# ScalarE's order written out in two MLPs, early loads of f, and sums of x pinned behind the last row block

## The chip, the core and the metric

The kernel runs on one core of a Trainium2 chip. Its engines are TensorE (PE; PEld are its weight loads), VectorE (DVE), ScalarE (ACT), GpSimd (POOL) and SyncE (SP), whose queue issues all DMAs here. The metric is the device time of one execution in microseconds (us), the median of several runs.

## The reference

Two decoder layers over 1024 tokens of width 1024 in float32. Each layer has a mixer (gated linear attention beside sparse attention in the first, a spatial-gating MLP in the second) and then a dense MLP of hidden width 4096. The change is in the two dense MLPs:

```python
def _squared_relu_mlp(x, w1, w2):
    h = jax.nn.relu(x @ w1)
    return (h * h) @ w2

f = _squared_relu_mlp(_rms_norm(h, norm_g[layer, 2]), ffn_w1[layer], ffn_w2[layer])
h = h + _rms_norm(f, norm_g[layer, 3])
```

## The kernel before

Every product is made in three passes of a high and a low part: `split` copies the high part with ScalarE (`acopy`, line 138) and takes the low part as a difference with VectorE (`sub`, line 148). A matmul has 128 x 128 weights and 512 columns; `mm` (line 162) records them all.

`ffn` (line 360) computes f = relu(x w1) squared and then f w2, both by a scheme of seven products in place of eight for 2 x 2 blocks (`SEVEN`, line 351). It has these stages:

- **The start.** The boundary of the stage before gives x in rows of 128 tokens, eight blocks, each normalised, transposed by TensorE and split into `xT`. The first four column blocks of w1 are multiplied in the plain way (`f1`, line 381), and meanwhile the sums of x that the seven products need are made from `xT`: `whole` (line 437) adds high and low part of a slice, `sums_y` (line 440) makes ten VectorE instructions for each of four slices k. `split1(2)` between them splits the third column block of w1.
- **The pair loop** (line 651), pairs q = 2 to 15 of column blocks of w1. A pair has seven units u = 0 to 6 (`unit1`, line 489) of 12 matmuls. The units of one pair share three banks; several units add onto a bank whose earlier value has been copied out by then: units 2 and 4 onto that of unit 0. ScalarE copies the banks of units 0, 2 and 3, and applies relu and square for unit 6; VectorE adds units 1, 4 and 5. In each unit the next pair's weights are prepared (`prep_pair`, line 470: a difference or sum where the scheme wants one, the ScalarE copy, the VectorE difference). `fetch_pair` (line 460) loads 1 MB of w1 for pair q+2, and `scale_pair` (line 465) multiplies it by the norm's gain, eight ScalarE copies, two each in units 3 to 6 by the code. Results go to DRAM (`fbuf`), with their sums (`sums_f`, line 514).
- **The second product** (line 693): 28 steps, a group of two pairs (steps 0 to 6) and three groups of four pairs, each with seven steps. A step multiplies four row blocks (`rows2`, line 592) and prepares the next step's weights and f (`prep2`, line 557). f comes back from DRAM through `fetch_f` (line 541) into a ring of five places, the weights through `fetch_w2` (line 548). Group 0 copies banks out with ScalarE or adds with VectorE, by the unit; the other groups add.
- **The end**: the plain product of the first four column blocks and the boundary to the next stage. Its operands come in through `of_last` (line 613).

The program is scheduled at build time. Each engine executes its queue in order; which instruction stands where in the queue is the scheduler's choice by its own clock, unless `tc.keep_in_program_order` pins an instruction behind the one traced before it on its engine. `keep` (line 143) does that while `fixed` is true, from the pair loop to the end of the second product. Before, TensorE's matmuls and VectorE's additions, differences and the relu-square step were pinned there; ScalarE's copies were not. DMA issues are pinned in neither kernel.

Of the kernel before, what the change touches and what calls it, by code (L numbers as in the profile page):

```python
# [117 lines left out]
def tile_trunk(ctx, tc, x, norm_g, ffn_w1, ffn_w2, e_w_in, e_w_out, gla_w_gate, gla_b_gate,  # L118
# [15 lines left out]

    act, dve, pool, pe = nc.scalar, nc.vector, nc.gpsimd, nc.tensor

    def acopy(o, i, **kw):
        act.activation(o, i, AF.Copy, **kw)  # L138


    fixed = [False]

    def keep(ins):
        if fixed[0]:
            tc.keep_in_program_order(ins)

    def sub(o, a, b):
        keep(dve.tensor_tensor(o, a, b, op=OP.subtract))  # L148
# [211 lines left out]
    def ffn(l, hsrc, hdst, gi, nxt):  # L360
# [74 lines left out]
        tmp = Ring(stg[4:] + [bnd.reg(o, 512) for o in (6, 8, 10, 12)])  # L435

        def whole(o, name, k):
            add(o.f, Y[name].f[:, 0, k], Y[name].f[:, 1, k])

        def sums_y(k):  # L440

# [47 lines left out]
        def unit1(q, u):  # L489
            x, y, which, begin, _, _ = SEVEN[u]  # L490
            b = 3 * (q % 2) + (0 if which == 0 else 1 if u == 1 else 2)
            w, xh = live(pairs[q, x]), Y[y]
            for k in range(4):
                for i, (a, v) in enumerate(PASS):
                    mm(bank[:, b, :], w.r[:, a, k, :], xh.r[:, v, k, :],
                       begin and k == 0 and i == 0, k == 3 and i == 2)
            pb = bank[:, b, :]
            if u in (0, 2, 3):
                hf[q, ("11", 0, "21", "22")[u]] = r = ring.next()
                acopy(r.f, pb)  # L500
            elif u == 6:
                hf[q, "12"] = r = ring.next()
                act.activation(r.f, pb, AF.Relu)
                act.activation(r.f, r.f, AF.Square)
                store(q, "12", r)
            else:
                name = {1: "11", 4: "22", 5: "21"}[u]
                r = live(hf[q, name])
                add(r.f, r.f, pb)
                keep(dve.scalar_tensor_tensor(r.f, r.f, 0.0, r.f, op0=OP.max, op1=OP.mult))  # L510
                if u != 5:
                    store(q, name, r)
# [13 lines left out]
        groups = [[2, 3]] + [list(range(4 + 4 * i, 8 + 4 * i)) for i in range(3)]  # L526
        wraw = [shaped(v, (2, 2, 512)) for v in (raw2, rawt)]
        T1 = [bnd.reg(o, 512) for o in (8, 10, 12, 6)]
        stage = Ring([bnd.reg(o, 512) for o in (14, 16, 0, 2, 4)])
        setA, setB = (X[h].ring(0, 8, 2, 512).views for h in range(2))  # L530
        setC = HS + [ws.reg(0, 2, 512)]
# [9 lines left out]
        def fetch_f():  # L541
            if len(loaded) < len(queue):
                q, name = queue[len(loaded)]
                r = stage.next()
                nc.sync.dma_start(r.f, frow(q, name))
                loaded.append(r)

# [9 lines left out]
        def prep2(g, u):  # L557

            slots = sets[g, u]
            for j, q in enumerate(groups[g]):  # L560
# [20 lines left out]
                def of_f(j=j):  # L581
                    o = slots[2 * j + 1]
                    src = loaded[taken[0]]
                    taken[0] += 1
                    yield from halves(live(src), o[:, 0], o[:, 1])
                    if (g, u) != (0, 0):
                        fetch_f()

                yield of_w()
                yield of_f()  # L590
# [59 lines left out]
        fixed[0] = True  # L650
        for q in range(2, NP):
            if q == NP - 1:
                for j in range(2):
                    for name in ("11", "12", "21", "22"):
                        fetch_w2(0, j, name)
                first = iter(list(prep2(0, 0)))
            for u in range(7):
                work = []
                if q + 1 < NP:
                    work.append(prep_pair(q + 1, u))  # L660
                elif u >= 3:
                    work.append(next(first))
                for w in work:
                    next(w)
                unit1(q, u)
                for w in work:
                    all_of(w)
                sums_f(q - 1 if u < 6 else q, u)
                if q == NP - 1 and u in (1, 2):
                    fetch_f()  # L670
                if u == 0:
                    fetch_pair(q + 2)
                if u >= 3:
                    scale_pair(q + 2, (2 * u - 6, 2 * u - 5))
# [1 line left out]
        acc = sb.F("acc", NT * D, slot="acc")  # L676
        acc_of = [acc.reg(4 * t, D) for t in range(NT)]
        wraw += [sa.F(f"w2raw{i}", 2, 2, 512, slot=f"w1{i}") for i in (1, 0)]
        for j in (2, 3):
            for name in ("11", "12", "21", "22"):  # L680
                fetch_w2(1, j, name)
        sums_f(NP - 1, 0)
        for _ in range(2):
            fetch_f()
        order = [(g, u) for g in range(len(groups)) for u in range(7)]
        ws2 = sb.R("w2b", 3 * D, slot="w2b")
        WS = ws.ring(0, 4, 2, 512).views + ws2.ring(0, 3, 2, 512).views
        wT = {(i // 2, i % 2): s for i, s in enumerate(WS + [HS[6]])}
        rest = [of_last(k, c, i) for i, k, c in
                [(i, "w", c) for c in range(2) for i in range(2)]  # L690
                + [(0, "h", c) for c in range(4)] + [(i, "w", c) for c in (2, 3) for i in range(2)]
                + [(1, "h", c) for c in range(4)]]
        for s, (g, u) in enumerate(order):
            steps = list(prep2(*order[s + 1])) if s + 1 < len(order) else []
            n = len(steps)
            for rb in range(4):
# [13 lines left out]
                    all_of(w)  # L710
                if s == 0 and rb == 0:
                    sums_f(NP - 1, 1)
                    for _ in range(5 - len(loaded) + taken[0]):
                        fetch_f()
        fixed[0] = False
        assert not rest
        load_gpost(gi + 1)
# [901 lines left out]
    i = 0  # L1619
# [50 lines left out]
```

## Time and profile before

| | us |
|---|---|
| median of three runs | 2587.97 (2586.36 to 2588.24) |
| the profiled execution | 2585.08 |
| its span | 2583.3 |
| TensorE busy | 2504.6 (97%) |
| VectorE busy | 1784.9 (69%) |
| ScalarE busy | 1280.9 (50%) |
| DMA, share of 16 engines | 33.3% |

A busy TensorE is not TensorE at its peak: matmuls overlap, one takes 393 ns in the record and a new one starts every 227 ns or so. What counts are the stretches in which it starts none. The first MLP lies from about 690 to 1385 us of the span, the second from about 1900 to the end.

### The profile page before, as it was taken

To read this page: it belongs to the slowest core of one execution; us is meant where nothing else is said; L and a number is where in the kernel's file an instruction comes from. 1 tells how busy PE (TensorE), PEld (TensorE's weight loads), DVE (VectorE), ACT (ScalarE), POOL (GpSimd) and SP (SyncE) were. 2 spreads that over 40 slices of the span, in tenths; PEclk is the share of its full clock that TensorE was granted. 3 is DMA by queue.
4 is the path that set the end of the run, shared out by engine and by line. 5 is a ranking of instruction groups with operands and counts; after the bars stand their busy time and mean duration, and the time that the engine had idled before them with its cause. 6 is when DMAs were issued, how large, how long until landed. Compare 5 with 4: busy or idle time off the path is not lost. (4 is left out here: it accounts for less than half of the span.)

```text
span 2583.3 us, 33390 instructions
## 1 busy us (share of the span) xinstructions
PE 2504.6 (97%) x12130; PEld 2086.6 (81%) x12130; DVE 1784.9 (69%) x3107; ACT 1280.9 (50%) x2503; POOL 297.8 (12%) x204
## 2 busy tenths in 40 slices
PE   8999999999999998999999999999999999999998
PEld 7888888888777777788887888888887777778886
DVE  5576478887776665887874248665667666588786
ACT  5656378787664444544454132233356544454442
POOL 2321122332400000000020011100020000000003
PEclk9999999999999999999999999999999999999999
DMA  4122110002534445454442111121243444544534
GB/s 131 51 66 81 58 41 34 25 18 90 188 106 139 135 144 203 131 163 163 138 157 98 33 42 41 41 82 49 74 139 106 135 139 142 202 136 162 162 122 163
DMA packets 191694, 279.56 MB, mean 108 GB/s; under 512 B 14388, under 2 KB 97576, under 8 KB 191528
## 3 DMA queue, kind: packets, MB, share of 16 engines
q1 hardware_dynamic: 191528, 277.42, 33.3%
q8 instruction: 95, 1.56, 0.2%
q14 instruction: 71, 0.58, 0.1%
HBM read 198.72 MB, written 78.64 MB: 107 GB/s over the span
## 5 line engine op out<-in xcount | busy, mean ns | idle before, releaser
L162 PE MATMUL bank<-base_x 128*128 128x512 f32 x1920 | 453.0, 393 | 14.6 <-ACT base_x L138 12.0
L162 PEld LDWEIGHTS bank<-base_x 128*128 128x128 f32 x1920 | 362.3, 189 | 97.7 <-ACT base_x L138 13.9
L154 DVE TENSOR_TENSOR ffb_acc<-ffb_acc,bank 128x512 f32<-128x512 f32 x224 | 152.9, 686 | 101.4 <-PE bank L162 100.1
L138 ACT ACTIVATE base_x<-base_bnd 128x512 fp32r<-128x512 f32 (+1 forms) x193 | 120.9, 639 | 184.3 <-DMA base_bnd<-fbuf 110.5
L162 PE MATMUL bank<-base_x,ffa_w 128*128 128x512 f32 x864 | 205.6, 395 | 3.5 <-ACT base_bnd L390 1.9
L162 PE MATMUL bank<-base_x,ffa_w1n 128*128 128x512 f32 x816 | 195.2, 394 | 2.0 <-DVE ffa_w1n L148 2.0
L162 PEld LDWEIGHTS bank<-base_x,ffa_w 128*128 128x128 f32 x864 | 163.6, 191 | 40.1 <-ACT base_bnd L390 2.8
L162 PE MATMUL bank<-base_x,mv_w 128*128 128x512 f32 x768 | 185.9, 393 | 0.8 <-DVE nsq_qq L1368 0.8
L260 POOL TENSOR_TENSOR ffb_acc<-ffb_acc,base_bnd 128x1024 f32<-128x1024 f32 x15 | 37.2, 2486 | 1277.5 <-ACT base_bnd L210 1269.2
L162 PEld LDWEIGHTS bank<-base_x,ffa_w1n 128*128 128x128 f32 x816 | 152.5, 189 | 33.4 <-DVE ffa_w1n L148 2.5
L162 PEld LDWEIGHTS bank<-base_x,mv_w 128*128 128x128 f32 x768 | 140.7, 188 | 28.4 <-DVE nsq_qq L1368 1.0
L148 DVE TENSOR_TENSOR base_x<-bank,base_x 128x512 fp32r<-128x512 f32 x204 | 135.5, 682 | 26.1 <-ACT base_x L138 24.9
L138 ACT ACTIVATE base_x<-bank 128x512 fp32r<-128x512 f32 x204 | 117.5, 598 | 50.1 <-PE bank L244 31.7
L148 DVE TENSOR_TENSOR base_x<-base_bnd,base_x 128x512 fp32r<-128x512 f32 (+1 forms) x185 | 127.2, 700 | 20.3 <-ACT base_x L138 20.3
L162 PE MATMUL bank<-base_x,ffb_hTb 128*128 128x512 f32 x480 | 111.7, 389 | 0.0
L162 PEld LDWEIGHTS bank<-base_x,ffb_hTb 128*128 128x128 f32 x480 | 90.1, 188 | 18.7
L162 PE MATMUL bank<-nsa_kk,nsq_qq 128*128 128x512 f32 (+3 forms) x384 | 94.4, 356 | 4.3 <-ACT base_bnd L1487 2.5
L1486 DVE TENSOR_REDUCE base_cf<-bank 128x1 f32<-128x640 f32 (+7 forms) x128 | 88.5, 698 | 13.1 <-PE bank L162 12.4
L162 PE MATMUL bank<-base_x,nsa_V 128*128 128x512 f32 x264 | 94.5, 431 | 2.6 <-DVE base_x L148 1.3
L138 ACT ACTIVATE ffa_raw<-ffa_raw,base_cf 128x256 f32<-128x256 f32 (+1 forms) x176 | 65.7, 457 | 57.4 <-DMA ffa_raw<-in_ffn_w_dram 57.4
L162 PE MATMUL bank<-ffa_hTa,base_x 128*128 128x512 f32 x384 | 92.9, 389 | 0.0
L154 DVE TENSOR_TENSOR sgu_v<-sgu_v,bank 128x512 f32<-128x512 f32 x96 | 64.6, 684 | 37.7 <-PE bank L162 37.3
(429 smaller groups left out, 5234.8 us busy)
## 6 DMA issues: line engine op xcount, KB each, us to landing
base_bnd<-fbuf SPq DMA_DIRECT2D x212, 256.0 KB, 2.7
fbuf<-base_bnd SPq DMA_DIRECT2D x134, 256.0 KB, 3.9
fbuf<-ffb_stg SPq DMA_DIRECT2D x78, 256.0 KB, 5.9
ffb_raw<-in_ffn_w_dram SPq DMA_DIRECT2D x14, 1024.0 KB, 6.8
ffa_raw<-in_ffn_w_dram SPq DMA_DIRECT2D x14, 1024.0 KB, 6.8
hbuf<-base_bnd SPq DMA_DIRECT2D x24, 512.0 KB, 3.3
ffa_w2raw<-in_ffn_w_dram SPq DMA_DIRECT2D x48, 256.0 KB, 2.7
base_bnd<-hbuf SPq DMA_DIRECT2D x24, 512.0 KB, 3.6
```

The source lines that it names most:

```text
L138: act.activation(o, i, AF.Copy, **kw)
L148: keep(dve.tensor_tensor(o, a, b, op=OP.subtract))
L154: keep(dve.tensor_tensor(o, a, b, op=OP.add))
L162: keep(pe.matmul(o, lhsT, rhs, start=start, stop=stop, skip_group_check=True))
L260: pool.tensor_tensor(acc, acc, gpost.f, op=OP.mult)
L1486: dve.reduce_max(out=nm, in_=sc[:, 0:W], axis=AX, negate=True)
```

## The change

The copies of `acopy` and ScalarE's relu and square in `unit1` are pinned in program order while `fixed` is true. The additions in `whole` are pinned always, so each stands behind everything traced before it on VectorE: the last row block of the boundary, the split of w1's first blocks, and within the sums whatever was traced between.

The first five blocks of f are loaded together after unit 1 of the last pair, into five places of their own (`first_at`: three regions of `bnd`, two of `stg`), instead of two there, two after the loop and three in the first step. Each preparation of a block of f, the first two included, then loads one more. The eight loads of w2 for the second half of group 1 move from behind the pair loop to the ends of steps 1 to 4, two each. The loads for group 0 are written by name first. The tile `w2b`, which takes the space of `stg`, is made at step 7.

```diff
-    def acopy(o, i, **kw):
-        act.activation(o, i, AF.Copy, **kw)
+    def acopy(o, i, **kw):
+        keep(act.activation(o, i, AF.Copy, **kw))
...
         def whole(o, name, k):
-            add(o.f, Y[name].f[:, 0, k], Y[name].f[:, 1, k])
+            tc.keep_in_program_order(dve.tensor_tensor(o.f, Y[name].f[:, 0, k],
+                                                       Y[name].f[:, 1, k], op=OP.add))
...
-                act.activation(r.f, pb, AF.Relu)
-                act.activation(r.f, r.f, AF.Square)
+                keep(act.activation(r.f, pb, AF.Relu))
+                keep(act.activation(r.f, r.f, AF.Square))
...
+        first_at = [bnd.reg(14, 512), bnd.reg(16, 512), bnd.reg(12, 512), stg[2], stg[3]]
         stage = Ring([bnd.reg(o, 512) for o in (14, 16, 0, 2, 4)])
...
-                r = stage.next()
+                r = first_at[len(loaded)] if len(loaded) < 5 else stage.next()
                 nc.sync.dma_start(r.f, frow(q, name))
...
-                    yield from halves(live(src), o[:, 0], o[:, 1])
-                    if (g, u) != (0, 0):
-                        fetch_f()
+                    yield from halves(src if taken[0] <= 5 else live(src), o[:, 0], o[:, 1])
+                    fetch_f()
...
-                for j in range(2):
-                    for name in ("11", "12", "21", "22"):
+                for name in ("11", "12", "22", "21"):
+                    for j in range(2):
                         fetch_w2(0, j, name)
...
-                if q == NP - 1 and u in (1, 2):
-                    fetch_f()
+                if q == NP - 1 and u == 1:
+                    for _ in range(5):
+                        fetch_f()
...
-        for j in (2, 3):
-            for name in ("11", "12", "21", "22"):
-                fetch_w2(1, j, name)
         sums_f(NP - 1, 0)
-        for _ in range(2):
-            fetch_f()
...
-        ws2 = sb.R("w2b", 3 * D, slot="w2b")
...
+            if s == 7:
+                ws2 = sb.R("w2b", 3 * D, slot="w2b")
...
                 if s == 0 and rb == 0:
                     sums_f(NP - 1, 1)
-                    for _ in range(5 - len(loaded) + taken[0]):
-                        fetch_f()
+            if 1 <= s <= 4:
+                for j in (2, 3):
+                    fetch_w2(1, j, ("11", "12", "22", "21")[s - 1])
```

## Rows read from the trace of the kernel before

**Rows 1.** TensorE's waits, whole span: who waited for whom, us, times, longest.
```profile
PE bank L162 <- ACT base_x L138: 12.2, 3, 6.0
PE bank L162 <- ACT ffb_stg L138: 11.7, 12, 1.5
```

**Rows 2.** Timeline of TensorE, pair loops, unit 4: start, length, what, idle before.
```profile
753.17 2.88 PE L162 MATMUL bank<-ffb_w2a,ffa_hTa 128*128 128x512 f32 x12
...
812.67 3.02 PE L162 MATMUL bank<-ffb_w2a,ffa_hTa 128*128 128x512 f32 x12 [0.81 <-ACT base_bnd L138]
...
994.57 2.88 PE L162 MATMUL bank<-ffb_w2a,ffa_w 128*128 128x512 f32 x12
...
1013.61 2.88 PE L162 MATMUL bank<-ffb_w2a,ffb_hTb 128*128 128x512 f32 x12
...
1981.48 2.88 PE L162 MATMUL bank<-ffb_w2a,ffb_hTb 128*128 128x512 f32 x12
...
2222.10 2.88 PE L162 MATMUL bank<-ffb_w2a,ffa_w 128*128 128x512 f32 x12
```

**Rows 3.** Timeline of the other engines, one pair of the first MLP.
```profile
801.54 0.38 SPq L462 DMA_DIRECT2D ffa_raw<-in_ffn_w_dram  x1
...
808.31 3.31 ACT L138 ACTIVATE ffa_raw<-ffa_raw,base_cf 128x256 f32<-128x256 f32 x8 [3.97 <-DMA ffa_raw<-in_ffn_w_dram]
...
809.07 0.68 DVE L148 TENSOR_TENSOR ffb_raw<-ffb_raw 128x512 f32<-128x512 f32 x1
...
812.04 0.57 ACT L138 ACTIVATE base_bnd<-bank 128x512 f32<-128x512 f32 x1
```

**Rows 4.** Timeline of TensorE, from the last pair to group 1.
```profile
1033.31 10.00 PE L162 MATMUL bank<-base_x 128*128 128x512 f32 x29 [5.94 <-ACT base_x L138]
...
1071.31 22.30 PE L162 MATMUL bank<-base_x 128*128 128x512 f32 x96
...
2298.08 22.30 PE L162 MATMUL bank<-base_x 128*128 128x512 f32 x96
```

**Rows 5.** Timeline of the transfer queue (SPq) and ScalarE in the first passage.
```profile
1018.69 0.32 SPq L545 DMA_DIRECT2D base_bnd<-fbuf  x1
1019.24 4.18 SPq L552 DMA_DIRECT2D ffa_w2raw<-in_ffn_w_dram  x6
...
1027.38 0.97 SPq L545 DMA_DIRECT2D base_bnd<-fbuf  x2
...
1032.63 1.24 ACT L138 ACTIVATE base_x<-base_bnd 128x512 fp32r<-128x512 f32 x2 [4.11 <-DMA base_bnd<-fbuf]
```

**Rows 6.** DMA issues of the page: count, KB each, median us to landing.
```profile
fbuf<-ffb_stg SPq DMA_DIRECT2D x78, 256.0 KB, 5.9
```

**Rows 7.** Stretches: busy us of PE, PEld, DVE, ACT, POOL, then PEclk, DMA, GB/s.
```profile
705.00:710.00 5.00, 4.36 (x10) 3.47 (x11) 4.96 (x9) 2.97 (x8) 0.00 (x0) 0.50 0.27 94
...
1035.00:1040.00 5.00, 5.00 (x13) 3.58 (x13) 3.33 (x7) 2.96 (x6) 0.00 (x0) 0.55 0.33 104
```

**Rows 8.** Timeline and stretches (as in rows 7) of the two MLPs' starts.
```profile
701.83 3.09 DVE L154 TENSOR_TENSOR ffb_stg<-base_x 128x512 f32<-128x512 f32 x5
...
702.34 0.60 ACT L138 ACTIVATE base_x<-bank 128x512 fp32r<-128x512 f32 x1 [1.04 <-PE bank L244]
...
705.64 14.06 PE L162 MATMUL bank<-base_x,ffa_w 128*128 128x512 f32 x48 [1.43 <-DVE base_x L148]
...
716.99 1.23 DVE L148 TENSOR_TENSOR ffa_w<-ffa_raw,ffa_w 128x1024 fp32r<-128x1024 f32 x1
...
747.55 3.06 PE L162 MATMUL bank<-ffb_yT,ffa_hTa 128*128 128x512 f32 x12
...
1947.47 1.22 DVE L148 TENSOR_TENSOR ffa_w<-ffa_raw,ffa_w 128x1024 fp32r<-128x1024 f32 x1
...
706.00:746.00 40.00, 39.05 (x160) 31.66 (x160) 35.96 (x58) 31.42 (x63) 0.00 (x0) 0.93 0.29 92
1937.00:1974.00 37.00, 35.87 (x157) 29.10 (x156) 34.88 (x55) 31.24 (x63) 0.00 (x0) 1.00 0.29 94
```

More of the change, by code (lines that the diff above doesn't have):

```diff
@@ L678, in ffn @@
         wraw += [sa.F(f"w2raw{i}", 2, 2, 512, slot=f"w1{i}") for i in (1, 0)]
-        for j in (2, 3):
-            for name in ("11", "12", "21", "22"):
-                fetch_w2(1, j, name)
         sums_f(NP - 1, 0)
-        for _ in range(2):
-            fetch_f()
         order = [(g, u) for g in range(len(groups)) for u in range(7)]
-        ws2 = sb.R("w2b", 3 * D, slot="w2b")
-        WS = ws.ring(0, 4, 2, 512).views + ws2.ring(0, 3, 2, 512).views
-        wT = {(i // 2, i % 2): s for i, s in enumerate(WS + [HS[6]])}
         rest = [of_last(k, c, i) for i, k, c in
@@ L693, in ffn @@
         for s, (g, u) in enumerate(order):
+            if s == 7:
+                ws2 = sb.R("w2b", 3 * D, slot="w2b")
+                WS = ws.ring(0, 4, 2, 512).views + ws2.ring(0, 3, 2, 512).views
+                wT = {(i // 2, i % 2): s for i, s in enumerate(WS + [HS[6]])}
             steps = list(prep2(*order[s + 1])) if s + 1 < len(order) else []
```

## The prediction, made before the changed kernel was run

> **What bounds the kernel now.** I read the page first: TensorE is busy for 97% of the span and the chain that ended last names the other engines with 1% and less, so the time is TensorE's own work plus the places where it runs dry. The list of TensorE's waits finds those [rows 1]: its two longest lines are ScalarE copies (line 138), and both lie in the two MLPs. The timeline of TensorE then shows three places in each MLP; the rest of the kernel is not touched by the change.
>
> *Place one, the pair loop.* A pair is seven units of 12 matmuls. No wait lies between the rows of 994.57 and 1013.61 [rows 2], and they are one pair apart: 19.04 us, 2.72 per unit. The twelve pairs before took 994.57 - 753.17 = 241.40 instead of 12 x 19.04 = 228.48, so 12.92 are lost. In the second MLP 2222.10 - 1981.48 = 240.62, and 12.14 are lost. The loss sits at one spot of a pair: unit 4 (`S3`) adds onto the bank of unit 2 and waits until ScalarE has copied that bank out. One case is in [rows 3]: the 1 MB load for a later pair is issued at 801.54, ScalarE stands idle for 3.97 us until 808.31 because eight scalings of that load are next in its queue, works on them for 3.3 us, and only then (812.04) copies the bank; TensorE, dry since 812.67 - 0.81 = 811.86, starts unit 4 at 812.67 [rows 2].
>
> *Place two, the passage to the second product.* From unit 4 of the last pair to group 1 there are 3 units and 7 steps of two units' length, 17 x 2.72 = 46.24 us. It took 1071.31 - 1013.61 = 57.70, and in the second MLP 2298.08 - (2222.10 + 19.04) = 56.94 [rows 2, 4]: losses of 11.46 and 10.70. The main piece is one idle time of 5.94 us before 1033.31; behind it 29 matmuls take 10.0 us where 6.6 would do. The transfer queue says why [rows 5]: block 2 of f (counted from 0) goes out at 1018.69, then come eight loads of the next group's weights (six in the row of 1019.24), and block 3, which the second step needs, goes out at 1027.38; ScalarE gets it at 1032.63. The granted clock then is 0.55 of full [rows 7].
>
> *Place three, the start of each MLP.* VectorE puts sums of x ahead of the last row block's two subtractions: five of them run from 701.83 to 704.9, 0.61 each, the subtractions follow, and TensorE goes on at 705.64 at half clock, 48 matmuls in 14.06 us where 10.88 would do [rows 7, 8].
>
> **Part one, ScalarE's written order in the pair loop.** Nothing is added or taken away; each copy stays where the code has it. The eight scalings then come two by two behind units 3 to 6. The load lands 6.8 us after its issue (801.54 to 808.31); unit 3 ends 10.3 us after it (811.86), so 3.5 us of cover stand against a late load. The new order queues the eviction of unit 2 behind the copy for `S3` of the next pair, which waits for a VectorE subtraction. That ends at 809.07 + 0.68 = 809.75; a copy (taken as 0.63) and the eviction (0.57) bring 811.05 with the hand-overs, 0.8 us before TensorE is dry at 811.86 [rows 3]. So unit 4 no longer waits. Unit 3's eviction sits behind one more such copy and is due a unit later. VectorE's order was fixed already; by the code it has 21 instructions a pair, 21 x 0.61 = 12.8 us of 19.04. I take the whole loss: **12.92 + 12.14 = 25.1 us**, which is also the upper bound. From below: if two instructions more (1.2 us) stand before the eviction than I count, 0.4 us come back in each of 26 pairs, with 0.3 of refill (idle 0.81 at 812.67, 1.1 over the period) 18 us, and 7 are left.
>
> **Part two, the five blocks of f.** They are issued after unit 1 of the last pair, into places whose last users are sums of f; the eight weight loads move behind steps 1 to 4, two each; and every f copy, the first two included, issues the next load. On the transfer queue block 3 then stands before 1018.69 instead of at 1027.38. The last of the five goes into a place (`stg[3]`) that has just been stored, so the queue waits for that store, 5.9 us by the page's median [rows 6]; next behind it is the store after unit 4, three units (8.2 us) later, so the wait is covered, and a store that is late by the rest is read by nobody for several steps. Each moved weight is wanted over 10 us after its load is issued (two steps). What is late next is VectorE: in step 1 it has four additions, four low parts and two differences, 10 x 0.61 = 6.1 us in a step of 5.44, the last low part queued behind the last addition, and I count it 0.9 us late for step 2; by the same count 0.4 late for steps 5 and 6, and 0.5 for group 1 (12 x 0.61 = 7.3 us of preparation in 5.44). With 0.3 of refill for each that is about 3.3 per MLP. Gain: 11.46 + 10.70 - 6.6 = **15.6 us**. Bounds: 22.2 with no rest at all; 5 if another wait takes most of the gap's place and keeps the clock down.
>
> The clock is in this sum: behind the gap of 5.94 us the granted clock fell to 0.55 of full (1.2 GHz for most of that stretch). The Trainium skill ("TensorE: Matmul & The Clock Gate", Part 1) says that the throttled state is the default and that activity releases it, with two levels only. The trace agrees, with 0.50 after the waits around 701 [rows 7]; by that rule a shorter gap that remained could still cost the slow level, which is the lower bound just given.
>
> **Part three, the sums of x.** Pinned behind everything VectorE was given before, they leave the last two subtractions alone: the first of them needs only ScalarE's copy (702.34 + 0.60 = 702.94 [rows 8]) and comes 2.0 us earlier; if TensorE's clock then stays up, 14.06 - 10.88 = 3.2 more. But the pin has a second end: the sums also stand behind the subtraction that splits the third column block of w1 (716.99 + 1.23 in the first MLP, 1947.47 + 1.22 in the second). By then I count 14 of the 40 instructions of `sums_y` done before; now the preparation of pair 2 can fill 3 or 4 of those places, so VectorE is some 10.5 x 0.61 = 6.4 us behind. Its idle time in these stretches is 40 - 35.96 = 4.0 and 37 - 34.88 = 2.1 us, and at 746 it is 3.6 us ahead of TensorE's need (unit 2's last quarter, 747.55 + 2.04 [rows 8]). The eviction of unit 0 now stands behind the last split of `T4`, too. First MLP: 6.4 - 4.0 - 2.0 = 0.4 late, within that room, so I let 1.5 of the 2.0 arrive. Second: 6.4 - 2.1 = 4.3 late with little gained ahead; 1.5 lost. Net **0**, from -5 (the idle times absorb little) to +6 (2.0 + 3.2 and a little in the second).
>
> **Sum.** 25.1 + 15.6 + 0 = 40.7 us. The profiled execution took 2585.1 (span 2583.3 and 1.8 around it); 2585.1 - 40.7 = 2544.4. It lies 2.9 below the median of the three runs, 2588.0, so against the median: **2547 us**.
>
> **Rivals.**
> *The pair wait moves instead of ending*: 7 instead of 25.1, 2588 - 7 - 15.6 = 2565. For it: 0.8 us is all the room that the eviction has. Against: each link of it is a row.
> *The passage gains only 5*: 2588 - 25.1 - 5 = 2558. For it: VectorE has more work than a step is long; against: only in three of the seven steps.
> *More*: the sums give 4 and the passage leaves little, 2588 - 25.1 - 19 - 4 = 2540.
> *Slower than before*: the subtraction that feeds the `S3` copy comes a unit later than in the trace, because the stores, reordered, hold the places that VectorE writes. In the written order the eviction of unit 2 then misses by 2.72 - 0.8 = 1.9 us in each of 26 pairs, 50 us in place of the 25.1 lost now: 2588 + 25 - 15.6 = 2597. It costs from 0.8 us of lateness on and makes the whole slower from 0.8 + 40.7 / 26 = 2.4. Against: the subtraction of 809.07 writes in place, no store holds it. Beside it a rule of the Trainium skill ("TensorE: Matmul & The Clock Gate", Architectural detail): ScalarE and VectorE are strict FIFOs, so an eviction can't pass a copy that waits. The trace agrees, as at 812.04 the eviction came after eight scalings.
> *The pins do not change the order that matters* (scalings still ahead of the eviction): 2588 - 15.6 = 2572.
>
> **How the numbers follow.** Forecast, 2541 to 2553: 0.58. More: 0.11. Passage only 5: 0.13. Pair wait moved: 0.09. Pins without effect: 0.03. Slower: 0.05. About no change, if two of these meet: 0.01. Leaving out the last three and the far ends, the range is 2537 to 2565. Faster by over 0.2% (5 us, about what a measurement of this kernel can tell): 0.93; within: 0.02; slower: 0.05.
>
> **What the profile of the changed kernel would show.** Part one: pairs 19.0 to 19.1 us apart, no ScalarE line among TensorE's waits inside the loop, scalings in twos; if a wait remains before unit 4, the copy that stands before the eviction is the culprit. Part two: five loads of f near unit 1 of the last pair, no idle time above 1 us in group 0, full clock there, VectorE as the releaser of what remains. Part three: the sums behind the last subtractions; the time from 705.64's successor to unit 2 tells which end of the pin wins. The prediction is wrong if ScalarE waits for a load in front of an eviction, or if VectorE's chain before unit 2 is over 3 us late.

## The result, and the profile after

| | before | after |
|---|---|---|
| median, us | 2587.8 (2586.4 to 2588.2) | 2551.0 (2547.5 to 2552.2) |
| profiled execution, us | 2585.1 | 2552.2 |
| its span, us | 2583.3 | 2550.4 |

The ratio after to before is 0.9857, 95% interval 0.984 to 0.9874: 36.8 us faster where 40.7 were forecast, and 2551 lies inside the range of 2537 to 2565. The sum came out nearly right, but two of its terms did not, with opposite signs. The profiles show it stage by stage (us, one execution each; the marks are starts of rows on TensorE's timeline):

| stage | before | after | gain |
|---|---|---|---|
| up to the transposes of the last row block but one, first MLP | 697.41 | 701.85 | -4.44 |
| from there to unit 4 of the first pair | 55.76 | 59.36 | -3.60 |
| pair loop: unit 4 of the first pair to unit 4 of the last | 260.44 | 247.52 | 12.92 |
| unit 4 of the last pair to group 1 | 57.70 | 48.45 | 9.25 |
| group 1 to the first transposes at the MLP's end | 259.53 | 256.52 | 3.01 |
| from there to the last transposes ahead of the second MLP | 602.80 | 602.19 | 0.61 |
| from there to unit 4 of the first pair | 47.84 | 56.25 | -8.41 |
| second pair loop | 259.66 | 247.52 | 12.14 |
| second passage to group 1 | 56.94 | 48.39 | 8.55 |
| group 1 to the first matmul of the plain product | 222.14 | 219.61 | 2.53 |
| from there to the end | 63.08 | 62.74 | 0.34 |
| sum | | | 32.90 |

The first line is not the change's: TensorE has the same instructions in the same order up to there in both, and the eleven kernels of the experiments below, with the pinned sums or without them, reach that mark at 697.6 to 699.9 us. The granted clock in one stretch of the mixer (250 to 300 us) was 0.93 in the changed kernel's execution and 1.00 in the other. Without this line the sum is 37.3, close to the 36.8 of the medians.

The two lines that end at unit 4 of the first pair each hold a gain and a loss. From the mark to unit 0 the changed kernel is faster, by 3.25 us in the first MLP (742.09 - 697.41 against 743.28 - 701.85) and 0.75 in the second; from unit 0 to unit 4 it is slower, by 6.85 and 9.16.

TensorE's waits in the changed kernel, the largest lines (who waited for whom, us, times, longest):

```profile
PE bank L162 <- ACT base_bnd L145: 11.6, 2, 6.9
PE bank L184 <- DMA base_bnd<-in_gla_norm_dram: 4.9, 1, 4.9
PE bank L162 <- DVE base_x L148: 4.3, 9, 1.5
```

Of the two lines of [rows 1] that of 11.7 us is gone, and that of 12.2 is down to 1.3. A new one stands on top: two waits, 11.6 us, for a bank copy by ScalarE. Where they are shows on TensorE's timeline (start, length, what, idle before), which answers [rows 2, 4, 8]:

```profile
743.28 5.60 PE L162 MATMUL bank<-base_x,ffa_hTa 128*128 128x512 f32 x24
753.60 5.05 PE L162 MATMUL bank<-ffb_yT,ffa_hTa 128*128 128x512 f32 x12 [4.72 <-ACT base_bnd L145]
...
761.21 2.88 PE L162 MATMUL bank<-ffb_w2a,ffa_hTa 128*128 128x512 f32 x12
780.25 2.88 PE L162 MATMUL bank<-ffb_w2a,ffa_w 128*128 128x512 f32 x12
...
989.69 2.88 PE L162 MATMUL bank<-ffb_w2a,ffa_w 128*128 128x512 f32 x12
...
1022.33 6.79 PE L162 MATMUL bank<-base_x 128*128 128x512 f32 x29
1029.79 15.50 PE L162 MATMUL bank<-base_x 128*128 128x512 f32 x67 [0.67 <-DVE base_x L148]
1046.68 4.64 PE L162 MATMUL bank<-ffa_hTa 128*128 128x512 f32 x19 [0.25 <-DVE ffa_hTa L148]
...
1963.83 8.48 PE L162 MATMUL bank<-ffb_yT,ffb_hTb 128*128 128x512 f32 x24 [6.89 <-ACT base_bnd L145]
1972.14 2.88 PE L162 MATMUL bank<-ffb_w2a,ffb_hTb 128*128 128x512 f32 x12
```

Unit 4 of the pairs: 761.21, 780.25 and so on to 989.69, 12 x 19.04 = 228.48 with no wait anywhere, where [rows 2] lost 12.92. The passage has no gap: 29 matmuls in 6.79 behind the unit before them, where [rows 4] had 5.94 of idle time and 10.0. And unit 2 of the first pair, which should follow unit 1 at 743.28 + 5.44 = 748.72, starts 4.9 us late, its 12 matmuls then taking 4.9 us instead of 2.7; in the second MLP it is 7.2 us late, and 24 matmuls take 8.3 instead of 5.4.

The stretch behind the first of these waits (as in [rows 7]) has the clock at 0.55, most of it at the lower of the two levels:

```profile
753.50:758.50 5.00, 4.90 (x13) 3.86 (x14) 4.24 (x8) 1.20 (x3) 0.00 (x0) 0.55 0.14 52
```

What made unit 2 wait stands in the timelines of VectorE and ScalarE:

```profile
705.42 2.49 DVE L438 TENSOR_TENSOR ffb_stg<-base_x 128x512 f32<-128x512 f32 x4
...
707.89 1.27 DVE L148 TENSOR_TENSOR base_x<-bank,base_x 128x512 fp32r<-128x512 f32 x2
...
715.25 1.29 DVE L148 TENSOR_TENSOR ffa_hTa<-ffb_raw,ffa_hTa 128x512 fp32r<-128x512 f32 x2 [5.96 <-ACT ffa_hTa L145]
...
719.41 1.23 DVE L148 TENSOR_TENSOR ffa_w<-ffa_raw,ffa_w 128x1024 fp32r<-128x1024 f32 x1 [1.05 <-ACT ffa_w L145]
720.55 0.68 DVE L438 TENSOR_TENSOR ffb_stg<-base_x 128x512 f32<-128x512 f32 x1
...
751.91 0.63 ACT L145 ACTIVATE base_x<-ffb_stg 128x512 fp32r<-128x512 f32 x1 [0.57 <-DVE ffb_stg L148]
752.45 0.61 ACT L145 ACTIVATE ffa_w<-ffa_raw 128x512 fp32r<-128x512 f32 x1
752.97 0.58 ACT L145 ACTIVATE base_bnd<-bank 128x512 f32<-128x512 f32 x1
```

Read from the bottom: the bank of unit 0 is copied out at 752.97, though it was full at about 746.0. Ahead of it in ScalarE's queue stands the last copy of T4 (751.91), which waits for VectorE's sums. And VectorE is late because it stood idle for 5.96 and 1.05 us: the first sum of `sums_y` (720.55) has to come behind the difference that splits the third column block of w1 (719.41). The rows show one thing more: the four sums of T4 (705.42) still run *ahead* of the last row block's two differences (707.89). In the kernel before, six sums ran there. The step that normalises that row block (L261) gives both timelines a common mark:

```profile
698.83 1.29 DVE L261 SCALAR_TENSOR_TENSOR base_bnd<-mv_P,base_cf,base_bnd 128x1024 f32<-128x1024 f32 x1 [1.12 <-POOL mv_P L260]
...
704.90 1.28 DVE L148 TENSOR_TENSOR base_x<-bank,base_x 128x512 fp32r<-128x512 f32 x2
```

```profile
703.02 1.28 DVE L261 SCALAR_TENSOR_TENSOR base_bnd<-mv_P,base_cf,base_bnd 128x1024 f32<-128x1024 f32 x1 [1.12 <-POOL mv_P L260]
```

The first two rows are of the kernel before, the third of the changed one. From the end of L261 to the end of the differences it is 6.1 us before (700.12 to 706.18) and 4.9 after (704.30 to 709.16), so 1.2 us were gained there. The other runs agree: 4.9 us in the seven kernels that have all the sums pinned (the changed one and six of the experiments), 6.1 in the four that have none (the kernel before and three). Unit 0 of the first pair then starts 36.8 to 39.1 us after L261 in the seven, 39.4 to 42.0 in the four, on average 2.3 us earlier. In the second MLP it starts 35.3 to 38.3 us after the last transposes in the seven and 35.9 to 36.1 in the four, which is no gain.

In the second MLP the chain has one link more, which the prediction does not have. The load for pair 4 goes out ahead of the load for pair 3 (1932.73 and 1933.87); the load for pair 3 lands 9.1 us after its issue, ScalarE waits 5.73 us for it, and VectorE behind ScalarE stands idle for 3.83:

```profile
1933.87 0.38 SPq L463 DMA_DIRECT2D ffa_raw<-in_ffn_w_dram  x1
...
1942.98 2.11 ACT L145 ACTIVATE ffa_raw<-ffa_raw,base_cf 128x256 f32<-128x256 f32 x5 [5.73 <-DMA ffa_raw<-in_ffn_w_dram]
...
1947.32 0.69 DVE L148 TENSOR_TENSOR base_x<-ffb_stg,base_x 128x512 fp32r<-128x512 f32 x1 [3.83 <-ACT base_x L145]
```

In the changed kernel without the pinned sums (below) that load goes out first (1922.97), and ScalarE waits 0.96 us for it. How much of the longer second wait this link makes was not tested by itself.

### The profile page after: what moved, and what is told of

It is laid out like the page before. It is cut to its first block, busy times and chain, and to the rows that moved or that the text cites. A ratio compares the mean times of both kernels' runs of the same rounds, so it can differ in the third digit from the quotient of the medians.

```text
span 2550.4 us, 33533 instructions
## 1 busy us (share of the span) xinstructions
PE 2492.9 (98%) x12130; PEld 2090.7 (82%) x12130; DVE 1793.7 (70%) x3107; ACT 1266.4 (50%) x2503; POOL 299.1 (12%) x204
## 5 line engine op out<-in xcount | busy, mean ns | idle before, releaser
L162 PE MATMUL bank<-base_x 128*128 128x512 f32 x1920 | 444.8, 389 | 1.5 <-DVE base_x L148 1.3
L260 POOL TENSOR_TENSOR ffb_acc<-ffb_acc,base_bnd 128x1024 f32<-128x1024 f32 x15 | 37.3, 2491 | 1241.7 <-ACT base_bnd L210 1233.5
L145 ACT ACTIVATE base_x<-base_bnd 128x512 fp32r<-128x512 f32 (+1 forms) x189 | 115.2, 634 | 65.3 <-DMA base_bnd<-fbuf 57.1
L1485 DVE TENSOR_REDUCE base_cf<-bank 128x1 f32<-128x640 f32 (+7 forms) x128 | 88.4, 697 | 11.6 <-PE bank L162 11.0
L154 DVE TENSOR_TENSOR sgu_v<-sgu_v,bank 128x512 f32<-128x512 f32 x96 | 64.7, 685 | 38.0 <-PE bank L162 37.3
L162 PE MATMUL bank<-base_x,ffa_hTa 128*128 128x512 f32 x384 | 89.7, 389 | 0.0
## 6 DMA issues: line engine op xcount, KB each, us to landing
base_bnd<-fbuf SPq DMA_DIRECT2D x208, 256.0 KB, 2.7
fbuf<-base_bnd SPq DMA_DIRECT2D x134, 256.0 KB, 4.0
fbuf<-ffb_stg SPq DMA_DIRECT2D x78, 256.0 KB, 5.6
ffa_w2raw<-in_ffn_w_dram SPq DMA_DIRECT2D x48, 256.0 KB, 2.6
```

Of the source, the lines that this page charges most:

```text
L145: keep(act.activation(o, i, AF.Copy, **kw))
L154: keep(dve.tensor_tensor(o, a, b, op=OP.add))
L162: keep(pe.matmul(o, lhsT, rhs, start=start, stop=stop, skip_group_check=True))
L260: pool.tensor_tensor(acc, acc, gpost.f, op=OP.mult)
L1485: dve.reduce_max(out=nm, in_=sc[:, 0:W], axis=AX, negate=True)
```

## The experiments

Each experiment is given with its median and its ratio to the kernel before, run on the same chip; the three of one execution have no ratio and are read by their profiles.

### One part alone, and all but one

**ScalarE's order alone**, in the kernel before:

```diff
-    def acopy(o, i, **kw):
-        act.activation(o, i, AF.Copy, **kw)
+    def acopy(o, i, **kw):
+        keep(act.activation(o, i, AF.Copy, **kw))
...
-                act.activation(r.f, pb, AF.Relu)
-                act.activation(r.f, r.f, AF.Square)
+                keep(act.activation(r.f, pb, AF.Relu))
+                keep(act.activation(r.f, r.f, AF.Square))
```

> The kernel before with ScalarE's order pinned in the MLPs and nothing else. My theory: the 25.1 us of the pair loops come from this part alone, and the small waits of groups 1 to 3 (3.0 and 2.9 us shorter in the changed kernel) go with it: 2588 - 25 - 6 = 2557, pairs 19.04 us apart, and no long wait before unit 2 of the first pair, since VectorE's sums stay ahead (the last split of T4 was copied at 743.63, the bank of unit 0 is full at about 744.8 in the trace before). Rival: the new wait before unit 2 (4.72 and 6.89 us in the changed kernel) belongs to this pin by itself, since it puts the bank copy of unit 0 behind the split of T4 in any case: then some 12 us come back, 2569.

Measured 2557.6 us, ratio 0.9873 (0.9857 to 0.9889): 32.6 us of gain. Both pair loops take 247.52 us, groups 1 to 3 take what they take in the changed kernel (256.57 us from group 1 to the first transposes, before 259.53; 219.57 in the second MLP to the plain product, before 222.14), and no wait stands before unit 2. So this part gives the 25.1 of the loops and the 5.5 of groups 1 to 3, and by itself it makes no new wait. The passage keeps its gap, 5.62 us.

**The early blocks of f alone** (that part of the diff, in the kernel before):

> The kernel before with the five early blocks of f and the moved weight loads alone; ScalarE's order and the sums as before. My theory: the passage to the second product gains what it gained in the changed kernel, 9.25 + 8.55 = 17.8 us, because the gap was a matter of the transfer queue alone: 2588 - 17.8 = 2570. Rival: part of that gain needs ScalarE's pinned order (its copies of f stand before the evictions there): then 5 to 10 us, 2578 to 2583, with a ScalarE line still among the waits of the passage.

Measured 2576.3 us, ratio 0.9947 (0.9934 to 0.996): 13.9 us. The answer lies between the two. The gap of 5.94 us is gone, the passages take 51.39 and 50.49 us, a gain of 6.31 and 6.45; the other 5 us need ScalarE's order as well. TensorE's timeline in the first passage:

```profile
1036.12 0.49 PE L162 MATMUL bank<-base_x 128*128 128x512 f32 x1 [0.65 <-ACT base_x L139]
1036.84 0.50 PE L162 MATMUL bank<-base_x 128*128 128x512 f32 x1 [0.23 <-DVE base_x L148]
1038.04 17.05 PE L162 MATMUL bank<-base_x 128*128 128x512 f32 x67 [0.70 <-DVE base_x L148]
```

Three small waits stand where the changed kernel has one, and the 67 matmuls behind them take 17.05 instead of 15.50.

**The pinned sums alone**, in the kernel before:

```diff
-            add(o.f, Y[name].f[:, 0, k], Y[name].f[:, 1, k])
+            tc.keep_in_program_order(dve.tensor_tensor(o.f, Y[name].f[:, 0, k],
+                                                       Y[name].f[:, 1, k], op=OP.add))
```

> The kernel before with the sums of x pinned behind the last row block and nothing else. My theory: the cost at the first pair needs two pins together, VectorE's sums that come late and ScalarE's queue that holds the bank copy of unit 0 behind the split of T4. Here ScalarE is free, so the gains at the start stay (3.25 + 0.75 us in the changed kernel) and unit 2 waits under 1 us for the last low part of T2: 2588 - 4 + 1 = 2585. Rival: the late sums alone make the wait (T2 and T4 themselves come too late for units 2 and 6): 4 to 8 us slower than before, 2592 to 2596.

Measured 2614.5 us, ratio 1.0101 (1.0085 to 1.0118): 24 us slower than before, which neither theory gave. From the last transposes to unit 4 the second MLP takes 54.28 (before 47.84), as the rival has it; but the larger part lies in the first pair loop, where the unpinned ScalarE loses 2 to 4 us in each pair instead of 1.1. TensorE, transfer queue and ScalarE in two pairs:

```profile
796.31 4.43 PE L162 MATMUL bank<-ffb_w2a,ffb_hTb 128*128 128x512 f32 x12 [1.76 <-ACT base_bnd L138]
819.21 3.02 PE L162 MATMUL bank<-ffb_w2a,ffa_hTa 128*128 128x512 f32 x12 [1.93 <-ACT base_bnd L138]
...
780.95 4.36 SPq L399 DMA_DIRECT2D fbuf<-base_bnd  x2
785.40 0.39 SPq L463 DMA_DIRECT2D ffb_raw<-in_ffn_w_dram  x1
...
792.47 3.30 ACT L138 ACTIVATE ffb_raw<-ffb_raw,base_cf 128x256 f32<-128x256 f32 x8 [5.45 <-DMA ffb_raw<-in_ffn_w_dram]
795.68 0.57 ACT L138 ACTIVATE base_bnd<-bank 128x512 f32<-128x512 f32 x1
```

It is the chain of [rows 3], with the load of w1 issued later. Unit 4 starts at 775.17 in the pair ahead, so unit 0 of this one at 783.5, and the load goes out 1.9 us after that, behind two stores that hold the queue from 780.95 on. In the pair of [rows 3] unit 0 starts at 800.82 and the load goes out 0.7 after it. So the load lands 9.0 us into the pair instead of 7.5, and the eight scalings and the bank copy come 1.5 us later too. In some pairs the clock falls as well (12 matmuls in 4.4). Here the first loop took 280.39 us where the kernel before took 260.44: it got worse by 20 us through a change outside it; with ScalarE pinned (the changed kernel has the same sums) it runs at 19.04.

**All but the pinned sums**, that is, the changed kernel with `add(...)` in `whole` again:

> The changed kernel with the sums of x left to the scheduler again; ScalarE's order and the early blocks of f stay. My theory: the pinned sums cost the changed kernel 16 us at the first pairs (6.85 + 9.16) and give 4 back at the starts; without them it is 12 us faster than the changed kernel: 2551 - 12 = 2539. Rival: ScalarE's pins keep the bank copy of unit 0 behind the split of T4 anyway, so that the wait before unit 2 stays and only the 4 us at the starts are lost: 2553 to 2555.

Measured 2538.9 us, ratio 0.98 (0.9781 to 0.9818): 12 us faster than the changed kernel. Unit 2 follows unit 1 at once in both MLPs (745.89 = 740.45 + 5.44 and, below, 1946.52 = 1941.08 + 5.44), and ScalarE copies the bank of unit 0 at 745.08:

```profile
745.08 0.60 ACT L145 ACTIVATE base_bnd<-bank 128x512 f32<-128x512 f32 x1 [1.08 <-DMA fbuf<-base_bnd]
...
1946.52 5.60 PE L162 MATMUL bank<-ffb_yT,ffb_hTb 128*128 128x512 f32 x24
```

From the same transposes to unit 4 this kernel takes 52.92 and 46.91 us, the changed one 59.36 and 56.25: 6.4 + 9.3 = 15.8 us in the profiles (this one was the fastest execution of the kernel), 12 by the medians and 15 by the ratios. The start, up to unit 0, takes 0.6 us more without the pins than with them in these two executions (698.44 to 740.45 against 701.85 to 743.28), and 2.3 us more on average over the kernels counted above, so what the pins give there is small against what they cost.

### Which end of the pin

**T4's splits behind units 2 and 3**, in the changed kernel:

```diff
-        for k in range(4):
-            split(T4f[k].f, Y["T4"][:, 0, k], Y["T4"][:, 1, k])
...
+                if q == 2 and u in (2, 3):
+                    for k in (2 * u - 4, 2 * u - 3):
+                        split(T4f[k].f, Y["T4"][:, 0, k], Y["T4"][:, 1, k])
```

> The changed kernel with the splits of T4 written behind units 2 and 3 of the first pair instead of ahead of the pair loop; the sums of x stay pinned. My theory: the wait before unit 2 is ScalarE's queue, in which the bank copy of unit 0 stands behind the last copy of T4. Without that, unit 2 waits only for the last low part of T2, 0.5 us in the first MLP (751.3 against 750.8) and 2.8 in the second (1961.5 against 1958.7): of the waits of 4.72 and 6.89 us and the slow matmuls behind them some 10 us come back, 2551 - 10 = 2541, and no bank copy is named before unit 2. Rival: VectorE's late sums alone hold unit 2 (or unit 6, which needs T4): then under 4 us come back, 2547 to 2551, with VectorE named.

Measured 2549.0 us, ratio 0.9837 (0.9824 to 0.9851): at most some 5 us come back, and the intervals overlap. From the same transposes to unit 4 the profiles have 59.00 and 54.94 us, the changed kernel 59.36 and 56.25: 1.7 us. The rival is right. TensorE and VectorE in the first MLP:

```profile
747.15 0.51 PE L162 MATMUL bank<-ffb_yT,ffa_hTa 128*128 128x512 f32 x1 [0.66 <-ACT ffb_yT L145]
750.71 1.22 PE L162 MATMUL bank<-ffb_yT,ffa_hTa 128*128 128x512 f32 x2 [3.05 <-DVE ffb_yT L148]
...
749.97 0.69 DVE L148 TENSOR_TENSOR ffb_yT<-ffb_stg,ffb_yT 128x512 fp32r<-128x512 f32 x1
```

With T4's copies out of the bank copy's way, unit 2 starts in time and stops before its last quarter, for T2's last low part: 0.66 + 3.05 in place of 4.72. ScalarE's queue showed the lateness, VectorE had it.

**The first slice free**, the pins kept on slices 1 to 3 only:

```diff
-            tc.keep_in_program_order(dve.tensor_tensor(o.f, Y[name].f[:, 0, k],
-                                                       Y[name].f[:, 1, k], op=OP.add))
+            ins = dve.tensor_tensor(o.f, Y[name].f[:, 0, k], Y[name].f[:, 1, k], op=OP.add)
+            if name != "21" and k > 0:
+                tc.keep_in_program_order(ins)
```

> The changed kernel with the sums of the first slice (k = 0) and the four of T4 left free; only the sums of slices 1 to 3 stay pinned. In the trace of the changed kernel VectorE stands idle for 5.96 us before 715.25, since the first sums of x are queued behind the split of the third column block of w1 (719.41), while the pins on the four sums of T4 hold nothing back (705.42, ahead of the last row block's two differences at 707.89). My theory: this one stretch of idle time is the whole lateness; with it filled, the last sums come some 6 us earlier, the wait before unit 2 goes, and the time is within 3 us of that without any pin on the sums: 2539 to 2542. Rival: the chain from slice to slice, each sum behind the previous slice's last difference, is what makes VectorE late: then at most a third of the 12 us comes back, 2547 or more.

Measured 2537.2 us, ratio 0.9795 (0.9782 to 0.9809): all of it comes back. VectorE, and unit 2 of the first pair:

```profile
701.83 3.09 DVE L438 TENSOR_TENSOR ffb_stg<-base_x 128x512 f32<-128x512 f32 x5
...
706.22 0.68 DVE L438 TENSOR_TENSOR ffb_stg<-base_x 128x512 f32<-128x512 f32 x1
...
746.52 2.88 PE L162 MATMUL bank<-ffb_yT,ffa_hTa 128*128 128x512 f32 x12
```

The sums of the first slice run from 706.22 on, in the time in which VectorE stood idle in the changed kernel, and unit 2 starts 5.43 us after unit 0, without a wait. So the cost of the pinned sums is in the first slice: its first sum behind the split of w1's third column block. The edges of the other slices cost next to nothing: in the second MLP unit 2 comes 0.9 us late, where it is not late without any pin, and the two medians can't be told apart. (T4's four sums are free in this kernel too. Pins on them alone were not run; that they hold nothing back is read from 705.42 and 707.89 above.)

**Sums really behind the last row block**, the pins on the sums taken out (`issue_after` puts what its block traces behind the instruction that it names, on that instruction's engine):

```diff
+            row_end[0] = split(pb.rearrange("p (k s) -> p k s", k=4),
...
+        with tc.issue_after(row_end[0].ins):
+            for k in range(4):
+                whole(T4f[k], "21", k)
...
+        with tc.issue_after(row_end[0].ins):
+            sums_y(0)
```

> The changed kernel with the pins on the sums of x taken out and the order that they were written for made directly: the four sums of T4 and the sums of the first slice stand behind the last row block's differences, the rest is free. My theory: the differences of the last row block come 2 to 3 us earlier in the first MLP and under 1 us earlier in the second, and nothing is late at the first pair: 2 to 4 us faster than without any pin, 2535 to 2537. Rival: five sums that come 3 us later push the whole chain of VectorE back and the wait before unit 2 returns: 2541 to 2546.

Measured 2538.0 us, ratio 0.9793 (0.978 to 0.9806), the same as without any pin (0.98). The wait of TensorE for the last row block's difference is gone in the first MLP (1.24 us without pins), but part of it is given back before unit 2, and in the second MLP more than was gained, 0.53 and 0.89 us: from the transposes to unit 4 it takes 52.37 and 48.17 us, without pins 52.92 and 46.91. VectorE has the order that was wanted, and TensorE the waits that came of it:

```profile
704.09 0.69 DVE L149 TENSOR_TENSOR base_x<-bank,base_x 128x512 fp32r<-128x512 f32 x1 [0.32 <-ACT base_x L146]
704.70 1.28 DVE L157 TENSOR_TENSOR ffb_stg<-base_x 128x512 f32<-128x512 f32 x2
...
744.83 3.02 PE L165 MATMUL bank<-ffb_yT,ffa_hTa 128*128 128x512 f32 x12 [0.53 <-ACT base_bnd L146]
...
1946.51 5.73 PE L165 MATMUL bank<-ffb_yT,ffb_hTb 128*128 128x512 f32 x24 [0.89 <-ACT base_bnd L146]
```

The aim of that part is worth nothing that can be measured, even where it is reached.

### The pair loop's mechanism and its room

**The bank of unit 2 copied four times**, in the changed kernel:

```diff
                 acopy(r.f, pb)
+                if u == 2:
+                    for _ in range(3):
+                        acopy(r.f, pb)
```

> The changed kernel in which ScalarE copies the bank of unit 2 four times instead of once (three copies of the same data more, about 0.48 us each). My theory: the bank of unit 2 is free 0.8 us before unit 4 needs it (893.69 against 894.49 in one pair), as the prediction had it; 3 x 0.48 = 1.44 us more make unit 4 wait 0.6 to 0.7 us in each pair, so pairs are 19.7 to 20.0 us apart and the kernel is 28 x 0.65 to 28 x 0.95 = 18 to 27 us slower than the changed one, 2569 to 2578. Rival: the room is larger than 1.4 us, since the copy only looks late when it has been waiting for nothing: pairs stay 19.04 us apart, 2551.

One execution took 2583.1 us. Unit 4 waits 0.98 us in every pair but the first and the last, and those pairs are 20.33 us apart:

```profile
797.24 3.06 PE L162 MATMUL bank<-ffb_w2a,ffb_hTb 128*128 128x512 f32 x12 [0.98 <-ACT base_bnd L145]
...
896.40 2.47 ACT L145 ACTIVATE ffb_stg<-bank 128x512 f32<-128x512 f32 x4
```

That makes 24 x 1.29 = 31 us, not 18 to 27, since a copy behind a copy of the same bank takes (2.47 - 0.57) / 3 = 0.63 and not 0.48, and since the 12 matmuls behind each wait take 0.3 us more than the wait itself (1.29 - 0.98). The room follows: 1.90 - 0.98 = 0.92 us, a little over the 0.8 of the prediction.

**The same bank copied twice** (`range(1)`):

> The changed kernel in which ScalarE copies the bank of unit 2 twice. With three copies more (0.63 us each by that run's trace, 1.90 together) unit 4 waited 0.98 us, so the room before unit 4 is about 0.9. My theory: one copy more, 0.63, is covered: pairs 19.04 us apart, no time lost, 2551. Rival: there is no such room and each copy costs its own share, 0.98 / 3 = 0.33 us and more in each of 28 pairs: 9 us or more, 2560.

One execution took 2553.9 us; pairs are 19.04 to 19.08 us apart, and the list of waits has none before unit 4. One more copy of 0.63 fits into 0.92, three more don't: the room is there, and it has an end.

**The eight scalings behind unit 1**, in the changed kernel:

```diff
-                if u >= 3:
-                    scale_pair(q + 2, (2 * u - 6, 2 * u - 5))
+                if u == 1:
+                    scale_pair(q + 2, range(KC))
```

> The changed kernel with the eight scalings of a load written behind unit 1 instead of two behind each of units 3 to 6: in the pinned order they now stand ahead of the bank copy of unit 2, as the scheduler had put them in the kernel before. My theory: that place alone made the loss of the pair loop. The load is issued at the start of unit 0 and lands about 7 us later, the scalings take 3.3, then come a copy and the bank copy, some 0.8 to 1.4 us after unit 4 could start: pairs 20.1 to 20.8 us apart, 24 pairs with a load, 26 to 42 us slower than the changed kernel, 2577 to 2593. Rival: it is the other copies' order that pinning mended; then pairs stay 19.04 us apart, 2551.

One execution took 2567.7 us: the waits come back, in 22 pairs, but smaller than I said; pairs are 19.5 to 20.7 us apart, and the loops take 255.9 and 256.0 us, 16.9 more together. ScalarE and TensorE in one pair:

```profile
811.13 3.31 ACT L145 ACTIVATE ffa_raw<-ffa_raw,base_cf 128x256 f32<-128x256 f32 x8 [2.89 <-DMA ffa_raw<-in_ffn_w_dram]
814.35 0.61 ACT L145 ACTIVATE ffa_w<-ffb_raw 128x512 fp32r<-128x512 f32 x1
814.87 0.58 ACT L145 ACTIVATE base_bnd<-bank 128x512 f32<-128x512 f32 x1
...
815.50 3.01 PE L162 MATMUL bank<-ffb_w2a,ffa_hTa 128*128 128x512 f32 x12 [0.25 <-ACT base_bnd L145]
```

It is the chain of [rows 3] again: a load that lands 6.8 us after its issue (804.33), eight scalings, a copy, the bank copy, unit 4. The place of the scalings ahead of the bank copy makes the wait, 16.9 of the 25.1 us; the other 8 are not assigned by a run. That the wait is smaller fits the load: it goes out 0.1 us after unit 0 begins (804.2), where the pair of [rows 3] has 0.7, so everything behind it is 0.6 us earlier, and the wait is 0.25 in place of 0.81.

### The moved weight loads

**The eight loads of w2 behind the pair loop again**, in the changed kernel:

```diff
+        for j in (2, 3):
+            for name in ("11", "12", "21", "22"):
+                fetch_w2(1, j, name)
         sums_f(NP - 1, 0)
...
-            if 1 <= s <= 4:
-                for j in (2, 3):
-                    fetch_w2(1, j, ("11", "12", "22", "21")[s - 1])
```

> The changed kernel with the eight loads of w2 written behind the pair loop again, as before; the five blocks of f stay early. My theory: the passage's gain is the early blocks alone. Loads are not pinned, and in the changed kernel's transfer queue five of the eight still stand where they stood, behind the fifth block of f: 2551 within 2 us, group 1 starting 48.4 us after unit 4 of the last pair. Rival: the moved loads free the queue for the next blocks of f, and without that a step waits for its block: 3 to 10 us slower, with a DMA or a ScalarE copy of f named in the passage.

Measured 2554.2 us, ratio 0.985 (0.9829 to 0.987), not to be told from the changed kernel's 0.9857, and the passage takes 48.39 us against 48.45. The changed kernel's transfer queue shows why:

```profile
1006.01 3.89 SPq L547 DMA_DIRECT2D ffb_stg<-fbuf  x2
...
1014.36 3.05 SPq L554 DMA_DIRECT2D ffa_w2raw<-in_ffn_w_dram  x5
...
1023.06 0.33 SPq L554 DMA_DIRECT2D ffa_w2raw<-in_ffn_w_dram  x1
```

The blocks of f in `stg` go out at 1006.01, where [rows 5] had block 3 at 1027.38. But five of the eight weight loads, written behind steps 1 to 4, still go out at 1014.36, in the last pair: nothing pins a load. That the scheduler put them where their places came free is a guess.

## Why the prediction was right, and where it was not

**Part one, right to the tenth.** The loops gave 12.92 + 12.14 = 25.06, the whole loss, and the room before unit 4 came out as worked out from [rows 3]: in the pair of 883 to 903 the bank copy ends at 893.69 and unit 4 starts at 894.49, 0.8 us later; by the copied bank it is 0.92. The rivals that live on that room (*the pair wait moves*, *slower than before*) were priced rightly in kind: four copies cost 32 us. What the step left out is the second product: "the rest of the kernel is not touched by the change" is wrong for groups 1 to 3, where ScalarE's copies of weights and f are pinned too. Small waits for them are gone, 3.01 + 2.53 = 5.5 us, all of it from this part by the run with it alone.

**Part two, right in size, by a step that was half wrong.** Predicted 15.6, measured 9.25 + 8.55 = 17.8. VectorE is what remains, as I wrote: waits of 0.67 in step 2 and 0.25 in steps 5 and 6, and 2.2 and 2.15 us in all where I counted 3.3. But the step says "the eight weight loads move behind steps 1 to 4"; five of them don't, and with all eight written back the passage is the same. What is left of this part is the early blocks of f, with the order of group 0's loads and the later `w2b`, which no run takes apart. And of the 17.8, the part alone brings 12.8: the last 5 need ScalarE's order, which the prediction gave to the loop alone. The clock's share was seen rightly: without the gap the 29 matmuls take 6.79 us, at a granted clock of 1.00.

**Part three, wrong.** Predicted 0, from -5 to +6; it cost 12 by the medians, 15 by the ratios, outside its bounds. The first step that failed is "pinned behind everything VectorE was given before, they leave the last two subtractions alone". A pin ties an instruction to the one traced directly before it on its engine, and only to that. The one traced directly before T4's sums is the split of w1's second block, long done; the last row block, traced earlier and not pinned itself, is free to come later, and it does (705.42, 707.89). So 1.2 of the 2.0 us counted there came, since four sums stand in front where six did. The section on the change says the same wrong thing of these pins. That unit 0 then starts some 2.3 us earlier, not far from the 1.5 that I let arrive, is luck: I had no sum left in front.

The step that made the loss is the balance for VectorE. "6.4 us behind" was right (idle 5.96 + 1.05 = 7.0), but I set three things against it: the idle time of the whole stretch, 4.0 and 2.1 us, the earlier start, 2.0, and 3.6 of room. The earlier start was no help, since it brings TensorE's need forward as well, and the idle time took up only part. In the first MLP the last copy of T4 comes 43.5 us after L261 before (743.63) and 47.6 after (751.91), so some 2.9 of the 7.0 were worked off; but unit 0 starts 3.0 us earlier after L261, and the copy stands 8.6 us behind that start in place of 1.5. Both of the prediction's signs of being wrong are there: VectorE's chain before unit 2 is over 3 us late (with T4's copies out of the way unit 2 still waits 3.05 us for it), and in the second MLP ScalarE waits for a load (5.73 us) in front of the copy of unit 0's bank. The third failure is the bank copy of unit 0 behind T4: I named it and gave it no price. It cost a little beyond VectorE's own lateness: with it out of the way the waits at unit 2 were 3.7 us in place of 4.7 and 4.7 in place of 6.9. The rule of the Trainium skill that the prediction set beside a rival ("TensorE: Matmul & The Clock Gate", Architectural detail: these engines are strict FIFOs) belonged here: the trace agrees, the bank was full at 746.0 and copied at 752.97, behind a copy that waited.

**The sum.** 25.1 + 17.8 + 5.5 + 0.9 (the two unnamed stretches of the table) - 12.0 = 37.3, by chance near 40.7: missed gains and a missed loss stood against each other. (The 12.0 are 4.0 gained up to unit 0 and 16.0 lost from there to unit 4.) The first four kernels bear the sum out on other ground: 32.6 and 13.9 for the two parts alone make 46.5, the two together 51. The pinned sums cost 24 us alone and 12 to 15 beside the other two. The parts don't add, since ScalarE's order changes what the other two are worth.

**What beats both kernels** is the change without its third part: 2538.9 us, ratio 0.98; the two kernels with fewer or other pins on the sums, 0.9795 and 0.9793, can't be told from it.

## What to carry to other kernels

An edge to the instruction traced directly before holds back what stands behind it, and lets everything traced earlier slide past, so look for the pinned instruction's neighbours in the new timeline before pricing what it should bring. Where an in-order queue copies out a bank that someone waits for, list what may stand ahead of it and what each of those waits for; a load that lands late, eight scalings behind it, then the copy, was worth 1% here, and fixing the order protected the loop from changes elsewhere. The idle time of a stretch absorbs an engine's lateness only in part, 2.9 of 7.0 us here, and what lets the engine that waits start earlier makes the lateness count for more.

## What the runs showed of the hardware

A copy of a bank directly behind another copy of the same bank into the same target starts 0.61 to 0.63 us after it (four copies in 2.47 us at 896.40), where copies between other places follow each other at 0.48 to 0.54 (751.91, 752.45 and 752.97 above): I had priced the extra copies at 0.48. Whether the bank or the target makes the difference is not shown. And waits of nearly one length cost TensorE different amounts. With the bank copied four times, each unit 4 waits 0.98 us and its 12 matmuls then take 3.02 to 3.06 with the clock at 1.00; with the pinned sums alone, waits of 1.76 to 2.11 us in the first MLP are followed by 12 matmuls in 3.0 to 3.1 us in six pairs and in 4.3 to 4.6 in five. The stretch behind two of them:

```profile
796.30:800.50 4.20, 4.19 (x12) 3.34 (x13) 2.44 (x4) 2.78 (x6) 0.00 (x0) 0.66 0.00 0
819.20:822.20 3.00, 2.99 (x13) 2.49 (x14) 1.39 (x2) 2.52 (x5) 0.00 (x0) 1.00 0.00 0
```

So the second price of a wait, 1.4 us of slow matmuls, comes or doesn't behind waits of the same length, and what decides it was not settled by these runs.
